# An encoder with routed experts: the router's products turned round, five weight tiles loaded earlier, the experts in another order

## The chip, the cores and the metric

The kernel runs on one core of a Trainium2 chip. The metric is the device time of one execution in microseconds (us), the median of several runs. Five engines share the work: PE multiplies matrices into eight banks of PSUM, DVE and ACT work elementwise, POOL sets zeros, SP issues the DMAs that bring weights from memory. Each engine runs its own instructions in order and waits on semaphores for the others.

## What is computed

Two layers; each adds a token mixer (four groups of heads, then `W_out`) to the 256 x 1024 activations and then a feed-forward part. In layer 0 that is dense, in layer 1 it is eight experts of which every token takes two:

```python
def reference(x, ...):
    for i in range(DEPTH):                                  # DEPTH = 2
        h = rms_norm(x, norm1_g[i])
        x = x + token_mixer(h, w_in[i], ..., w_out[i])      # 4 groups, group norm, @ w_out
        h = rms_norm(x, norm2_g[i])
        x = x + (swiglu(h, ffn_w_gate[0], ffn_w_up[0], ffn_w_down[0]) if i % 2 == 0 else
                 moe_swiglu(h, moe_w_router[0], moe_w_gate[0], moe_w_up[0], moe_w_down[0]))
    return rms_norm(x, final_norm_g)

def moe_swiglu(x, w_router, w_gate, w_up, w_down):          # x: 256 x 1024, 8 experts of 3584
    logits = xt @ w_router
    top_v, top_i = lax.top_k(logits, 2)
    gates = jax.nn.softmax(top_v, axis=-1)
    combine = sum(one_hot(top_i, 8) * gates[..., None], axis=1)
    for e in range(8):
        y = y + combine[:, e:e+1] * ((silu(xt @ w_gate[e]) * (xt @ w_up[e])) @ w_down[e])
    return y
```

All is float32. The eight experts' weights are 352 MB of the 423 MB that the kernel reads.

## The kernel before

**The recorded part.** Layers 0 and 1 up to the router are recorded first, and a planner (class `Plan`) then sets the order of the instructions on each engine by its own costs and by how many buffers of each kind there are; L532 is the line at which all of them are emitted. Weights that need full float32 precision are split by `split` into a rounded part `hi` (ACT) and a rest `lo` (DVE), from a tile `w` of 128 x 2048, and PE multiplies `hi` and `lo` by the parts of the activations. There are four `hi` buffers, three `lo` and one more of them (`lox`), 26 buffers `u` for everything of 128 x 512, and 8 PSUM banks `m`. In layer 1's `W_out`, group 0's weights are used whole, the other three groups' are split, two splits a group; each split feeds twelve matmuls of 512 columns.

**The router** (L1436). x is transposed by PE (four times four 128 x 128 blocks), ACT and DVE copy the transposed blocks `hT` out of PSUM, and 16 products with the eight columns of `W_router` (times the norm's weight: `wg`) give the logits in bank `lg`: `hT` is the stationary operand, `wg` the moving one. Then come a comparison on DVE for expert 0, a product `pos0` that counts tokens, a one-hot matrix `oh`, and the gather products `ga` of expert 0. Between them `idle` puts products that nobody reads.

**The experts' weights.** A tile is 128 x 4096 (2 MB). A ring of NRING = 10 tiles takes them in turn, so tile k may be issued when the last reader of tile k - 10 is done. Three buffers `r` lie where the state space tables of the mixer lay (L673, `opener`) and can be filled once these are read for the last time; five buffers `q` lie where `w`, `hi` and `lo` lay (L681, `opener_q`) and can be filled after `W_out`'s last matmul; two more belong to the experts' part. An expert has 21 tiles: seven column blocks in four units (2, 2, 2 and 1), each with gate `eg`, up `eu` and down `ed`. SP issues in the order in which the tiles are used. Units overlap: PE does `eg` and `eu` of one unit and then `ed` of the unit before.

**The experts' order.** The experts are ranked by their number of tokens, expert 0 always first. Ranks 1 to 4 (`WIDE`) have room for 96 tokens, here called B; the others, S, for 64. B's further 32 tokens are multiplied apart (`egx`, `ex`), while the weights are the same 21 tiles. `GROUPS` sets the order and which experts are gathered together (`gather`: at most 256 columns); the next group's gather runs during the last unit of the group before. It is 0 | 1, 5, 2 | 3, 6, 4 | 7, that is S | B S B | B S B | S. After each expert its result is added to x by the `sca` products.

Of the kernel before, what the change touches and what calls it, by code (L numbers as in the profile page):

```python
# [10 lines left out]
F32 = mybir.dt.float32  # L11
F32R = mybir.dt.float32r
# [6 lines left out]
P = 128  # L19
# [12 lines left out]
NE = 8  # L32
# [5 lines left out]


WIDE = (1, 2, 3, 4)  # L40
GROUPS = ((0,), (1, 5, 2), (3, 6, 4), (7,))

NU = 26
EXTRA = (0, 0, 1)
ZORDER = (("cf", "ssm", "qk", "vb", "cx"), ("cf", "qk", "vb", "ssm", "cx"))
GORDER = ((2, 0, 1, 3), (0, 2, 3, 1))
LATE = ()
# [7 lines left out]
FRONT = 3  # L55
FIRST = 0
URGENT = 30000.0
NR = 3
NQ = 5
NRING = 10  # L60
NHI = 4
NLO = 3
LATER = (1, 3)
TURN = 3
LEAD = 2
# [470 lines left out]
def build(tc, a, dbg=None, upto=99):  # L536
# [21 lines left out]
    def bank(name):  # L558
        if plan.open:
            return plan.buf("m", name)  # L560
        return ps.tile([P, 512], F32, tag="m", name=name)
# [15 lines left out]
        return sm.tile([P, 8], F32, tag="tiny", name=name, bufs=8)[:, :n]  # L577

    lasts = {}

    def in_turn(what, op):

# [8 lines left out]

    def split(src, parts=1):
        n = src.free_size()
        if plan.open:
            hi, lo = plan.buf("hi", "hi"), plan.buf("lo", "lo")
        else:
            hi = hl.tile([P, 1024], F32R, tag="hi", name="hi", bufs=NHI)
            lo = hl.tile([P, 1024], F32R, tag="lo", name="lo", bufs=NLO)
        hi, lo = hi[:, :n], lo[:, :n]
        for i in range(0, n, n // parts):  # L600
            c = slice(i, i + n // parts)
            in_turn("split", A.activation(hi[:, c], src[:, c], AF.Copy))
            V.tensor_tensor(lo[:, c], src[:, c], hi[:, c].bitcast(F32), ALU.subtract)
        return hi, lo
# [42 lines left out]
    def idle(after, columns):  # L647

        for n in columns:
            PE.matmul(bank("idle")[:, 0:n], ident, cst[:, 0:n], start=True, stop=True)  # L650
            plan.after(plan.ops[-1], after)
# [19 lines left out]
    right = []  # L671

    def opener():  # L673
# [4 lines left out]
            s.tile = right[0].tile([P, 4096], F32, tag=f"r{i}", name="r")  # L678
        plan.kinds["oh"][0].tile = right[0].tile([P, 4 * P], F32R, tag="oh", name="oh")

    def opener_q():  # L681

        pw.close()
        pool = ctx.enter_context(tc.tile_pool(name="qp", bufs=1, side="right", reuse_waits="tile"))
        right.append(pool)
        for i, s in enumerate(plan.kinds["q"]):
            s.tile = pool.tile([P, 4096], F32, tag=f"q{i}", name="q")
# [3 lines left out]
    def kind(name, n, w, dt=F32, pool=hp, tag=None, **kw):  # L691
        plan.kind(name, [pool.tile([P, w], dt, name=f"{name}{i}", **({"tag": tag} if tag else {}), **kw) for i in range(n)])
# [2 lines left out]
    hl = pw.enter_context(tc.tile_pool(name="hl", bufs=4))  # L695
    ring = pw.enter_context(tc.tile_pool(name="ring", bufs=4))
    kind("w", 4, 2048, pool=ring, tag="w")
    kind("hi", NHI, 1024, F32R, hl, "hi", bufs=NHI)
    kind("lo", NLO, 1024, F32R, hl, "lo", bufs=NLO)
    kind("m", 8, 512, F32, ps, "m")  # L700
    for n, w, dt, more in (("w", 2048, F32, EXTRA[0]), ("hi", 1024, F32R, EXTRA[1]), ("lo", 1024, F32R, EXTRA[2])):
        plan.more(n, [hl.tile([P, w], dt, name=f"{n}x{i}", tag=f"{n}x{i}", bufs=1) for i in range(more)])
    tables = {"el": 4096, "qr": 2048, "qi": 2048, "mt": 2048}
    for n, w in tables.items():
        kind(n, 1, w, pool=sx)
# [1 line left out]
        kind(n, 1, KD * S, F32R, top)  # L707
    plan.later("r", NR, plan.like["el"], opener)
    plan.later("oh", 1, plan.like["hi"][:, 0:4 * P], opener)
    plan.later("q", NQ, plan.like["el"], opener_q)  # L710
    kind("j", 1, 512, BF16, sm, "junk", bufs=1)
    u = lambda i: hp.tile([P, 576], F32, name="u", tag=f"u{i}")
# [266 lines left out]
    def mixer(L, T, late):  # L979
# [367 lines left out]
        groups = {}  # L1347
        for gi, f in ((3, state_space), (2, conformer), (0, attention), (1, short_conv)):
            groups[gi] = f()
        for gi in GORDER[L]:  # L1350
            group_out(gi, groups[gi])
        for t in range(2):
# [83 lines left out]
    def router():  # L1436
# [4 lines left out]
        plan.after(plan.ops[-1], early["router"])  # L1441
        wg = u2("wgr", 64).rearrange("p (k e) -> p k e", e=NE)
        V.tensor_tensor(wg, wr, g2.unsqueeze(2).to_broadcast([P, KD, NE]), ALU.mult)
        bl = bank("lg")
        copies, rest, logits = [], [], []
        for t in range(2):
            for h in range(2):
                b = bank("hT")
                with plan.one():
                    for k in range(4):  # L1450
                        c = (4 * h + k) * P
                        PE.transpose(b[:, k * P:(k + 1) * P], x[:, t, c:c + P], ident)
                turned = plan.ops[-1]
                hT = u2("hT")
                copies.append(V.tensor_copy(hT, b) if HT[2 * t + h] == "V" else A.activation(hT, b, AF.Copy))
                with plan.one():
                    for k in range(4):
                        PE.matmul(bl[:, t * NE:(t + 1) * NE], hT[:, k * P:(k + 1) * P], wg[:, 4 * h + k],
                                  start=(h + k == 0), stop=(h + k == 4))
                logits.append(plan.ops[-1])  # L1460
                hs = slice(512 * h, 512 * h + 512)
                rest.append(A.activation(h_hi[:, t, hs], x[:, t, hs], AF.Copy))
                V.tensor_tensor(h_lo[:, t, hs], x[:, t, hs], h_hi[:, t, hs].bitcast(F32), ALU.subtract).tail = URGENT - 1500.0
# [3 lines left out]
            plan.after(op, copies[-1])  # L1467
        lg, sel = lgs[:, 0], lgs[:, 1]
        te = lambda v: v.rearrange("p (t e) -> p t e", t=2)
        V.tensor_copy(lg, bl[:, 0:16])  # L1470

        gt0, s0, q0 = u2("gt0", 16), tiny(2, "s0"), tiny(2, "q0")
# [1 line left out]
        V.tensor_tensor(te(gt0), te(lg), te(lg)[:, :, 0:1].to_broadcast([P, 2, NE]), ALU.is_gt)  # L1474
        V.tensor_reduce(s0, te(gt0), AX.X, ALU.add)
        V.tensor_scalar(s0, s0, 1.5, None, ALU.is_lt)
        idle(logits[-1], (256, 256))
        bp_ = bank("pos0")
        with plan.one():
            PE.matmul(bp_[:, 0:1], C["tri"], s0[:, 0:1], start=True, stop=True)  # L1480
# [36 lines left out]
            plan.after(op, picked)  # L1517
        parts = [x for u in range(2) for x in up_parts(weights_of(0), u)]
        w0 = []
        for i, (n, src) in enumerate(parts[:NR + NQ]):  # L1520
            w0.append(plan.keep(plan.buf("r" if i < NR else "q", n)))
            kinds = tables if i == 0 else ("w", "hi", "lo") if i == NR else ()
            held = [op for op in plan.ops if any(b.kind in kinds for b in op.bufs)]
            op = SY.dma_start(w0[i], src)
            in_turn("load", op)
            for o in held:
                plan.after(op, o)
        return h_hi, h_lo, oh, w0

    def moe(h_hi, h_lo, oh0, w0, posm, comb, rst, lgs):  # L1530
# [4 lines left out]
        ring2 = pool("ring2", 1)  # L1535
        bp = pool("bp", 1)
        b2 = pool("b2", 2)
        rp, rq = right
        g2r = g2.real()
        nring = [0]  # L1540

        def weights(parts, pieces=1):

            ws = []
            for name, src in parts:
                n, i = nring[0], nring[0] % NRING
                nring[0] += 1
                if n < len(w0):
                    ws.append(w0[n])
                    continue  # L1550
                if i < NR:
                    w = rp.tile([P, 4096], F32, tag=f"r{i}", name=name)
                elif i < NR + NQ:
                    w = rq.tile([P, 4096], F32, tag=f"q{i - NR}", name=name)
                else:
                    w = ring2.tile([P, 4096], F32, tag=f"w{i}", name=name)
                n = pieces if src is parts[-1][1] else 1
                for k in range(n):
                    c = slice(4096 // n * k, 4096 // n * (k + 1))
                    SY.dma_start(w[:, c], src[:, c])  # L1560
                ws.append(w)
            return ws
# [538 lines left out]
```

## Time and profile before

| | |
|---|---|
| median of 3 runs | 1325.83 us (1325.54 to 1326.10) |
| the profiled execution | 1324.34 us, of which the span of the trace is 1322.6 us |
| PE busy | 1276.5 us (97%) |
| weight loads on PE | 765.0 us (58%) |
| DVE, ACT busy | 476.2 us (36%), 295.9 us (22%) |
| DMA | 423.32 MB, 320 GB/s over the span, 425 to 428 GB/s in most of the 40 slices after 490 us |
| granted TensorE clock | 0.984 of full speed |

The recorded part with the router takes the first 491 us, the eight experts run to 1306 us, and the final norm and the output take the rest. An instruction on PE counts as busy from its start to its modelled end, so a share of busy time says little on how fast PE goes; what a stretch lost is seen by setting it beside the same work elsewhere in the trace. Lines of the kernel are given as L532; L221 is the line at which all calls outside the recorded part are made. `q` tiles, once refilled, bear the names of what is in them (`eg`, `eu`, `ed`).

### The profile page before, as it was taken

The numbers are of one execution on the slowest core, as the hardware profiler recorded it, in microseconds if no ns is written. First come the engines' busy times: TensorE is split into PE (matmuls) and PEld (weight loads), VectorE is DVE, ScalarE is ACT, GpSimd is POOL, SyncE is SP. The second block draws the span as 40 slices with busy tenths as digits, with TensorE's granted clock in tenths as the row PEclk, the third lists the DMA queues.
The fourth block names the chain that finished last, engine by engine and source line by source line (L and its number), as shares of the span: only waits on it lengthen the run. The fifth ranks groups of instructions, "written<-read, shape, count | busy, mean of one in ns | idle before, by whom it ended". The sixth has DMA issues, their size and how long they took to land.

```text
span 1322.6 us, 23222 instructions
## 1 busy us (share of the span) xinstructions
PE 1276.5 (97%) x10172; PEld 765.0 (58%) x10173; DVE 476.2 (36%) x1059; ACT 295.9 (22%) x479; POOL 2.2 (0%) x25
## 2 busy tenths in 40 slices
PE   7999999999999999999999979999999999999995
PEld 6787799999888783444453324454445343445332
DVE  7999899855688852001001001001100100100102
ACT  4065644444535531001001000010100100100101
POOL 0000000000000000000000000000000000000000
PEclk9999899999999979999999989999999999999998
DMA  8214244555546569999999999999999999999994
GB/s 273 108 65 151 97 160 166 188 191 189 180 139 144 224 255 427 427 427 425 425 426 426 428 426 426 425 426 396 384 380 427 427 426 427 425 427 425 427 425 164
DMA packets 45923, 423.32 MB, mean 320 GB/s; under 512 B 12024, under 2 KB 14968, under 8 KB 16888
## 3 DMA queue, kind: packets, MB, share of 16 engines
q1 hardware_dynamic: 45816, 421.77, 78.5%
q8 instruction: 82, 1.34, 0.4%
q14 instruction: 25, 0.20, 0.0%
HBM read 420.21 MB, written 1.54 MB: 319 GB/s over the span
## 4 chain that ended last, share of the span: by engine, by line
PE 80%; DMA 11%; DVE 6%; ACT 2%; issue 1%; SPq 0%; DVEq 0%; ACTq 0%
PE m L532 29%; PE egu L221 25%; PE ea L221 11%; DMA eu<-in_moe_w_up 8%; PE egx L221 7%; PE ex L221 4%; DVE u L532 3%; DMA ed<-in_moe_w_down 3%; PE aT L221 1%; PE ga L221 1%; PE sca L221 1%; DVE t L532 1%; DVE lo L532 1%; ACT u L532 0%; ACT j L532 0%
## 5 line engine op out<-in xcount | busy, mean ns | idle before, releaser
L221 PE MATMUL ea<-ed,af 128*64 128x512 f32 x896 | 207.5, 602 | 3.5 <-DMA ed<-in_moe_w_down 3.5
L221 PE MATMUL egu<-eu,ef 128*64 128x512 f32 (+1 forms) x960 | 189.7, 537 | 5.1 <-DMA eu<-in_moe_w_up 5.1
L221 PE MATMUL egu<-eg,ef 128*64 128x512 f32 (+1 forms) x960 | 190.4, 540 | 3.6 <-DMA eg<-in_moe_w_gate 3.5
L221 DVE SCALAR_TENSOR_TENSOR sg<-egu,rs,sg 128x512 f32<-128x512 f32 (+1 forms) x32 | 21.9, 684 | 415.5 <-PE egu L221 399.6
L221 PEld LDWEIGHTS egu<-eg,ef 128*64 128x64 f32 x960 | 70.3, 138 | 116.9 <-issue 103.8
L221 PEld LDWEIGHTS egu<-eu,ef 128*64 128x64 f32 x960 | 69.8, 137 | 115.1 <-issue 96.8
L532 PE MATMUL m<-hlo,hi 128*128 128x256 f32 x480 | 134.7, 281 | 1.3 <-DVE hlo L532 1.3
L532 PE MATMUL m<-hh,hi 128*128 128x256 f32 x480 | 135.5, 282 | 0.0
L532 ACT ACTIVATE hi<-w 128x1024 fp32r<-128x1024 f32 x98 | 103.7, 1059 | 107.7 <-PE m L532 107.2
L221 PEld LDWEIGHTS ea<-ed,af 128*64 128x64 f32 x896 | 60.8, 137 | 113.4 <-issue 109.1
L532 DVE TENSOR_TENSOR lo<-w,hi 128x1024 fp32r<-128x1024 f32 x74 | 90.2, 1223 | 42.0 <-ACT hi L532 40.9
L532 PE MATMUL m<-hh,lo 128*128 128x256 f32 x364 | 102.2, 281 | 0.0
L532 PE MATMUL m<-hi,u 128*128 128x512 f32 x288 | 95.6, 398 | 0.0
L532 PEld LDWEIGHTS m<-hlo,hi 128*128 128x128 f32 x480 | 91.1, 190 | 2.1 <-DVE hlo L532 1.5
L532 PEld LDWEIGHTS m<-hh,hi 128*128 128x128 f32 x480 | 90.9, 189 | 1.0 <-issue 0.4
L532 DVE TENSOR_TENSOR u<-u 128x512 f32<-128x512 f32 (+5 forms) x136 | 78.8, 617 | 6.4 <-ACT u L532 4.8
L221 ACT ACTIVATE af<-aT 128x512 f32<-128x512 f32 (+2 forms) x48 | 21.4, 480 | 237.4 <-PE aT L221 237.4
L221 ACT ACTIVATE sg<-egu,rs 128x512 f32<-128x512 f32 (+1 forms) x32 | 20.3, 634 | 230.7 <-PE egu L221 230.7
L532 PEld LDWEIGHTS m<-hh,lo 128*128 128x128 f32 x364 | 69.2, 190 | 0.0
L532 PEld LDWEIGHTS m<-hi,u 128*128 128x128 f32 x288 | 54.5, 189 | 11.4 <-ACT hi L532 0.2
L532 DVE SCALAR_TENSOR_TENSOR u<-u,pp 128x256 f32<-128x256 f32 (+1 forms) x142 | 59.0, 481 | 1.5 <-ACT u L532 1.3
L532 PE MATMUL m<-u,w 128*128 128x256 f32 x256 | 58.7, 381 | 0.0
(194 smaller groups left out, 1324.0 us busy)
## 6 DMA issues: line engine op xcount, KB each, us to landing
ed<-in_moe_w_down SPq DMA_DIRECT2D x55, 2048.0 KB, 27.0
eg<-in_moe_w_gate SPq DMA_DIRECT2D x52, 2048.0 KB, 27.5
eu<-in_moe_w_up SPq DMA_DIRECT2D x52, 2048.0 KB, 30.7
w<-in_w_in SPq DMA_DIRECT2D x18, 1024.0 KB, 5.2
w<-in_ffn_w_gate SPq DMA_DIRECT2D x11, 1024.0 KB, 4.7
w<-in_ffn_w_up SPq DMA_DIRECT2D x11, 1024.0 KB, 5.1
w<-in_ffn_w_down SPq DMA_DIRECT2D x11, 1024.0 KB, 4.8
w<-in_w_out SPq DMA_DIRECT2D x8, 1024.0 KB, 5.2
```

Source lines behind the costliest of these rows:

```text
L221: return f(*[real(v) for v in a], **{k: real(v) for k, v in kw.items()})
L532: f(*[real(v) for v in a], **{k: real(v) for k, v in kw.items()})
```

## The change

Four things are changed.

1. In the router `wg` becomes the stationary operand (8 columns) and `hT` the moving one (128 columns), so the logits come out transposed, 8 x 256, in bank `lgT`. DVE copies each half to `lT`, and PE transposes it back into `lg`. One more pair of `idle` products is put in.
2. The buffers for the experts' first eight tiles are four `r`, one `p` and three `q` instead of three `r` and five `q`. `p` lies where a second set of split buffers (`hib`, `lob`) lies, which is given up earlier than the rest.
3. The split buffers become two sets of two (`hi`, `lo` and `hib`, `lob`) that `split` uses in turn; once layer 1's mixers are recorded (`few`), only the first set is used, so its `W_out` has two `hi` and two `lo`. There are 24 buffers `u` instead of 26, and the extra `lo` is gone.
4. `GROUPS` becomes 0 | 1, 2, 5 | 3, 6, 4 | 7, that is S | B B S | B S B | S.

```diff
-GROUPS = ((0,), (1, 5, 2), (3, 6, 4), (7,))
+GROUPS = ((0,), (1, 2, 5), (3, 6, 4), (7,))
-NU = 26
-EXTRA = (0, 0, 1)
+NU = 24
-NR = 3
-NQ = 5
+NR = 4
+NP = 1
+NQ = 3
-NHI = 4
-NLO = 3
+NSPLIT = 2
...
     def split(src, parts=1):
         n = src.free_size()
-        if plan.open:
-            hi, lo = plan.buf("hi", "hi"), plan.buf("lo", "lo")
-        else:
-            hi = hl.tile([P, 1024], F32R, tag="hi", name="hi", bufs=NHI)
-            lo = hl.tile([P, 1024], F32R, tag="lo", name="lo", bufs=NLO)
-        hi, lo = hi[:, :n], lo[:, :n]
+        kind_ = "" if len(few) > 0 else "ab"[nsplit[0] % 2].replace("a", "")
+        nsplit[0] += 1
+        hi, lo = plan.buf("hi" + kind_, "hi")[:, :n], plan.buf("lo" + kind_, "lo")[:, :n]
...
+    def opener_p():
+        pwb.close()
+        pool = ctx.enter_context(tc.tile_pool(name="pp", bufs=1, side="right", reuse_waits="tile"))
+        right.append(pool)
+        for i, s in enumerate(plan.kinds["p"]):
+            s.tile = pool.tile([P, 4096], F32, tag=f"p{i}", name="p")
...
+    pwb = ExitStack()
+    hlb = pwb.enter_context(tc.tile_pool(name="hlb", bufs=NSPLIT))
+    kind("hib", NSPLIT, 1024, F32R, hlb, "hib", bufs=NSPLIT)
+    kind("lob", NSPLIT, 1024, F32R, hlb, "lob", bufs=NSPLIT)
...
             groups[gi] = f()
+        few.extend([L] * L)
         for gi in GORDER[L]:
             group_out(gi, groups[gi])
...
-        bl = bank("lg")
+        bl, blT, lT = bank("lg"), bank("lgT"), u2("lT", 256)
...
-                        PE.matmul(bl[:, t * NE:(t + 1) * NE], hT[:, k * P:(k + 1) * P], wg[:, 4 * h + k],
-                                  start=(h + k == 0), stop=(h + k == 4))
+                        PE.matmul(blT[0:NE, t * P:(t + 1) * P], wg[:, 4 * h + k], hT[:, k * P:(k + 1) * P],
+                                  start=(h + k == 0), stop=(h + k == 4), skip_group_check=True)
...
+        for t in range(2):
+            V.tensor_copy(lT[0:NE, t * P:(t + 1) * P], blT[0:NE, t * P:(t + 1) * P])
+            if t:
+                idle(logits[-1], (256, 256))
+            PE.transpose(bl[:, t * NE:(t + 1) * NE], lT[0:NE, t * P:(t + 1) * P], ident[0:NE, 0:NE])
+        turned_back = plan.ops[-1]
         V.tensor_copy(lg, bl[:, 0:16])
...
-        idle(logits[-1], (256, 256))
+        idle(turned_back, (256, 256))
...
-        for i, (n, src) in enumerate(parts[:NR + NQ]):
-            w0.append(plan.keep(plan.buf("r" if i < NR else "q", n)))
-            kinds = tables if i == 0 else ("w", "hi", "lo") if i == NR else ()
+        for i, (n, src) in enumerate(parts[:NR + NP + NQ]):
+            w0.append(plan.keep(plan.buf("r" if i < NR else "p" if i < NR + NP else "q", n)))
+            kinds = {0: tables, NR: ("hib", "lob"), NR + NP: ("w", "hi", "lo")}.get(i, ())
```

Since the planner runs anew with other numbers of buffers, the order changes in many places of the recorded part. Three of them are shown.

SP's issues at the end of the recorded part, before (`r` and `q` are the experts' first tiles, `wr` is `W_router`, `ed` the first tiles of the two buffers of the experts' part):

```order
L532 DMA w_85<-in_w_out 128x2048
L532 DMA r<-in_moe_w_gate 128x4096 x2
L532 DMA r<-in_moe_w_up 128x4096
L532 DMA wr<-in_moe_w_router 128x8x8
L532 DMA q<-in_moe_w_up 128x4096
L532 DMA q<-in_moe_w_gate 128x4096 x2
L532 DMA q<-in_moe_w_up 128x4096 x2
L221 DMA ed<-in_moe_w_down 128x4096 x2
```

and of the changed kernel:

```order
L531 DMA w_85<-in_w_out 128x2048
L531 DMA r<-in_moe_w_gate 128x4096 x2
L531 DMA r<-in_moe_w_up 128x4096 x2
L531 DMA wr<-in_moe_w_router 128x8x8
L531 DMA p<-in_moe_w_gate 128x4096
L531 DMA q<-in_moe_w_gate 128x4096
L531 DMA q<-in_moe_w_up 128x4096 x2
L220 DMA ed<-in_moe_w_down 128x4096 x2
```

The tiles are the same and stand in the same order; five instead of three are in buffers that do not wait for the end of `W_out`.

ACT's last instructions of layer 1's `W_out`, before (`hi<-w` is the first half of a split; the number behind `hi` is the buffer, that behind `w` the tile of weights):

```order
L532 ACTIVATE hi_90<-w_87 128x1024
L532 ACT_TABLE_LOAD
L532 ACTIVATE u<-m_96,pp 128x256 x2
L532 ACTIVATE u<-u 128x512
L532 ACTIVATE u<-u,pp 128x256 x2
L532 ACTIVATE hi_91<-w_87 128x1024
L532 ACTIVATE u<-u 128x512
L532 ACTIVATE hi_89<-w_85 128x1024
L532 ACTIVATE u<-u,pp 128x256 x2
L532 ACTIVATE hi_88<-w_85 128x1024
L532 ACTIVATE u<-u,pp 128x256 x2
L532 ACTIVATE hh_108<-x 128x512 x2
```

and of the changed kernel:

```order
L531 ACT_TABLE_LOAD
L531 ACTIVATE u<-m_99,pp 128x256 x2
L531 ACTIVATE u<-u 128x512
L531 ACTIVATE u<-u,pp 128x256 x2
L531 ACTIVATE u<-u 128x512
L531 ACTIVATE hi_89<-w_87 128x1024
L531 ACTIVATE u<-u,pp 128x256 x2
L531 ACTIVATE hi_88<-w_87 128x1024
L531 ACTIVATE hi_89<-w_85 128x1024
L531 ACTIVATE u<-u,pp 128x256 x2
L531 ACTIVATE hi_88<-w_85 128x1024
L531 ACTIVATE hh_111<-x 128x512 x2
```

The last four splits had four buffers and have two; the first of them moved behind the work for the group's norm.

PE at the router, before (`m<-cst,x` are the transposes of x, `m<-u 128x8` the products for the logits, `m<-cst` the products that nobody reads, `m<-t,cst` is `pos0`; behind the arrow the moving operand stands first):

```order
L532 MATMUL m_99<-cst,x 128x128 x4
L532 MATMUL m_98<-u 128x8 x16
L532 MATMUL m_102<-cst 128x256
L532 MATMUL m_101<-cst 128x256
L532 MATMUL m_97<-t_152,cst 128x1 x3
L532 MATMUL m_95<-cst 128x128
L532 MATMUL m_96<-cst 128x128
L221 MATMUL ga<-oh,x 128x64 x14
```

and of the changed kernel:

```order
L531 MATMUL m_105<-cst,x 128x128 x4
L531 MATMUL m_101<-u 8x128 x16
L531 MATMUL m_102<-cst,u 128x8
L531 MATMUL m_103<-cst 128x256
L531 MATMUL m_102<-cst,u 128x8
L531 MATMUL m_106<-cst 128x256
L531 MATMUL m_100<-cst 128x256
L531 MATMUL m_99<-cst 128x256
L531 MATMUL m_104<-t_155,cst 128x1 x3
L531 MATMUL m_105<-cst 128x128
L531 MATMUL m_101<-cst 128x128
L220 MATMUL ga<-oh,x 128x64 x14
```

Ahead of `pos0` there stand two small transposes and four instead of two products that nobody reads. (An operation of this list on float32 shows as two instructions in the trace.)

## Rows read from the trace of the kernel before

**Rows 1.** Windows, one expert each: engines' busy us (instructions), PEclk, DMA share, GB/s.

```profile
490.99:570.15 79.16, 79.16 (x420) 32.05 (x420) 12.58 (x55) 7.05 (x12) 0.00 (x0) 0.98 1.01 426
570.15:689.21 119.06, 117.45 (x1183) 53.27 (x1182) 8.34 (x16) 8.75 (x19) 0.00 (x0) 1.00 1.01 426
689.21:776.70 87.49, 83.15 (x441) 30.95 (x438) 7.12 (x11) 6.53 (x12) 0.00 (x0) 0.98 1.01 426
776.70:901.79 125.09, 121.14 (x1159) 55.39 (x1158) 11.95 (x23) 8.75 (x19) 0.00 (x0) 0.99 1.01 426
901.79:1019.63 117.84, 117.84 (x1223) 54.83 (x1221) 9.21 (x18) 9.58 (x21) 0.00 (x0) 1.00 0.94 393
1019.63:1099.36 79.73, 79.73 (x441) 30.06 (x437) 7.12 (x11) 6.53 (x12) 0.00 (x0) 1.00 1.01 426
1099.36:1220.56 121.20, 118.88 (x1160) 55.49 (x1159) 9.64 (x19) 8.75 (x19) 0.00 (x0) 1.00 1.01 426
1220.56:1306.33 85.77, 85.77 (x480) 34.43 (x476) 7.28 (x12) 6.53 (x12) 0.00 (x0) 1.00 0.93 393
```

**Rows 2.** The chain that ended last, experts: start us, us, what.

```profile
589.21 7.04 PE egx L221 x128
...
797.53 7.04 PE egx L221 x128
...
896.30 2.08 PE ga L221 x16
...
903.68 1.33 PE rs L221 x53
...
917.17 7.04 PE egx L221 x128
...
964.93 13.73 PE egu L221 x64
...
1077.79 31.73 DMA eu<-in_moe_w_up
...
1116.65 7.04 PE egx L221 x128
```

**Rows 3.** The page's costliest groups on PE: busy us, mean ns, idle before, releaser.

```profile
L221 PE MATMUL ea<-ed,af 128*64 128x512 f32 x896 | 207.5, 602 | 3.5 <-DMA ed<-in_moe_w_down 3.5
L221 PE MATMUL egu<-eu,ef 128*64 128x512 f32 (+1 forms) x960 | 189.7, 537 | 5.1 <-DMA eu<-in_moe_w_up 5.1
L221 PE MATMUL egu<-eg,ef 128*64 128x512 f32 (+1 forms) x960 | 190.4, 540 | 3.6 <-DMA eg<-in_moe_w_gate 3.5
```

**Rows 4.** SP's timeline at layer 1's W_out: start us, us, issue.

```profile
440.19 1.31 SPq L532 DMA_DIRECT2D r<-in_moe_w_gate  x2
...
474.67 0.33 SPq L532 DMA_DIRECT2D q<-in_moe_w_up  x1
```

**Rows 5.** The page's split groups on ACT and DVE: busy us, mean ns, idle before.

```profile
L532 ACT ACTIVATE hi<-w 128x1024 fp32r<-128x1024 f32 x98 | 103.7, 1059 | 107.7 <-PE m L532 107.2
...
L532 DVE TENSOR_TENSOR lo<-w,hi 128x1024 fp32r<-128x1024 f32 x74 | 90.2, 1223 | 42.0 <-ACT hi L532 40.9
```

**Rows 6.** PE's timeline, end of W_out and router: start us, us, operation.

```profile
471.31 0.39 PE L532 MATMUL m<-lo,u 128*128 128x512 f32 x1
...
474.03 0.39 PE L532 MATMUL m<-lo,u 128*128 128x512 f32 x1
...
476.23 3.64 PE L532 MATMUL m<-u 128*128 128x8 f32 x32
...
479.72 1.11 PE L532 MATMUL m<-cst 128*128 128x256 f32 x4
...
482.85 6.08 PE L221 MATMUL ga<-oh,x 128*128 128x64 f32 x28
```

**Rows 7.** Windows at the router, columns as in rows 1.

```profile
474.26:481.00 6.74, 6.74 (x56) 6.28 (x55) 3.78 (x9) 5.51 (x13) 0.00 (x0) 1.00 0.82 297
481.00:494.70 13.70, 13.70 (x58) 11.11 (x59) 4.82 (x31) 1.96 (x3) 0.00 (x0) 0.50 1.01 429
```

More of the change, by code (lines that the diff above doesn't have):

```diff
@@ L579, in build @@
     lasts = {}
+    nsplit, few = [0], []
     def in_turn(what, op):
@@ L697, in build @@
     kind("w", 4, 2048, pool=ring, tag="w")
-    kind("hi", NHI, 1024, F32R, hl, "hi", bufs=NHI)
-    kind("lo", NLO, 1024, F32R, hl, "lo", bufs=NLO)
+    kind("hi", NSPLIT, 1024, F32R, hl, "hi", bufs=NSPLIT)
+    kind("lo", NSPLIT, 1024, F32R, hl, "lo", bufs=NSPLIT)
+    pwb = ExitStack()
+    hlb = pwb.enter_context(tc.tile_pool(name="hlb", bufs=NSPLIT))
+    kind("hib", NSPLIT, 1024, F32R, hlb, "hib", bufs=NSPLIT)
+    kind("lob", NSPLIT, 1024, F32R, hlb, "lob", bufs=NSPLIT)
     kind("m", 8, 512, F32, ps, "m")
-    for n, w, dt, more in (("w", 2048, F32, EXTRA[0]), ("hi", 1024, F32R, EXTRA[1]), ("lo", 1024, F32R, EXTRA[2])):
-        plan.more(n, [hl.tile([P, w], dt, name=f"{n}x{i}", tag=f"{n}x{i}", bufs=1) for i in range(more)])
     tables = {"el": 4096, "qr": 2048, "qi": 2048, "mt": 2048}
@@ L709, in build @@
     plan.later("oh", 1, plan.like["hi"][:, 0:4 * P], opener)
+    plan.later("p", NP, plan.like["el"], opener_p)
     plan.later("q", NQ, plan.like["el"], opener_q)
@@ L1537, in moe @@
         b2 = pool("b2", 2)
-        rp, rq = right
+        rp, rp2, rq = right
         g2r = g2.real()
@@ L1552, in weights @@
                     w = rp.tile([P, 4096], F32, tag=f"r{i}", name=name)
-                elif i < NR + NQ:
-                    w = rq.tile([P, 4096], F32, tag=f"q{i - NR}", name=name)
+                elif i < NR + NP:
+                    w = rp2.tile([P, 4096], F32, tag=f"p{i - NR}", name=name)
+                elif i < NR + NP + NQ:
+                    w = rq.tile([P, 4096], F32, tag=f"q{i - NR - NP}", name=name)
                 else:
```

## The prediction

> **What bounds the kernel now.** I read first the windows that hold one expert each [rows 1]. The column DMA share stands at 1.01 and the last column at 426 GB/s in all but two, so the stream of weights never pauses while the experts run; a tile of 2,097 KB takes 4.92 us and an expert's 21 tiles 103.4 us. PE needs less than that for an S (79.73 us where nothing was late, the window from 1019.63) and more for a B (117.84, from 901.79). So neither engine bounds the stage by itself: during an S the weights are late, during a B they run ahead until the ring of ten tiles is full. (In the last window, also at 393, the stream ends.) The reader is to see both in two odd windows: S from 689.21 lasts 87.49 instead of 79.73, and in the second of the two adjacent B's the stream falls to 393 GB/s, which is 117.84 x 33/426 = 9.1 us of lost transfer.
>
> The chain [rows 2] then says how long PE waited. A B's first gate and up products last 13.73 us, and 15.38 where the small `rs` products lie among them (901.79 to 917.17). The other three B's took 19.06 (570.15 to 589.21, with `rs`), 20.83 (776.70 to 797.53) and 17.29 (1099.36 to 1116.65, both without): waits of 3.7, 7.1 and 3.6 us. With the S's 87.49 - 79.73 = 7.8 that is 22.2 us of waiting for weights.
>
> The idle column shows only 3.5 + 5.1 + 3.6 = 12.2 us of it [rows 3], because a matmul that waits can count as busy. The Trainium skill warns of this (Perfetto Trace Analysis, Identifying the Most-Contended Engine): busy time of matmuls is a poor measure of how near PE is to its limit. By the 97% busy share and that column, weights that are never late would be worth 12.2 us at most; by the windows it is 22.2. The trace agrees with the rule, and I go by the windows.
>
> **Order and early tiles, together.** The instructions of an expert stay the same; what moves is when its weights are there. Before, SP issued three tiles at 440 us and the other five at 474.67, after `W_out`'s last matmul [rows 4]. Five tiles take 24.6 us and the gap is 34.5, so two more tiles fit in, and the stream of the experts stands 2 x 4.92 = 9.8 us further at any moment at which nothing holds it back. The first B, which waited 3.7 us, then waits no more, with 6 us to spare.
>
> PE's ledger, with the first product at 490.99 as before: S 79.16; B 119.06 - 3.7 = 115.4; second B 117.84 - 1.3 = 116.5, since `rs` (1.33) falls away inside a group [rows 2]. That ends at 802.1. Is the stream in front by then? By itself it would have 5 + (802.1 - 474.67)/4.92 = 71.5 tiles, with 63 used. In the kernel before, the tile for which the last B waited (the 130th, landed at 1077.79 + 31.73 = 1109.52) landed 89.9 us or 18.3 tiles after the end of the adjacent B's at 1019.63, so 111.7 had landed there with 105 used: 6.7 ahead is what the ring allows. 8.5 is more; the ring is full here too, and the stream leaves 802.1 as it left 1019.63. From there the same tile of the next B (after one S) lands at 802.1 + 89.9 = 892.0; PE, with the gather that now stands in that S (2 x 2.08, [rows 2]), asks for it at 802.1 + 83.9 + 8.5 = 894.5 (8.5 is 15.38 less half of 13.73), so nothing is late. B 115.4 and S 79.7 bring PE to the last B at 1081.1 and to its up products at 1088. Their tile lands 42 tiles after 892.0, at 1098.6, and PE waits 10.6 us. Before, it landed at 1109.5. What follows (this B, the last S, the norm) is unchanged, so this part is worth **-10.9 us**. Everything up to 802.1 is PE alone; whatever moves the first product at 490.99 moves the end by as much.
>
> **Split buffers in `W_out`.** Four splits there now share two buffers. While PE uses one buffer's twelve matmuls, 2.72 us (471.31 to 474.03, [rows 6]), the other must be filled: ACT 1.06 and DVE 1.22 us, 2.28 [rows 5], plus two hand-overs and whatever DVE and ACT do between. It nearly fits. Bounds: 0 if it fits, 4 x 2.28 = 9.1 if each split is waited for whole. I take **+2**, half a microsecond each. It delays `q` and the first product alike.
>
> **Router.** The loads of 128 stationary columns go, and 128 moving columns come. Before, 32 instructions took 3.64 us, 0.114 each; of 256 columns one takes 1.11/4 = 0.28 [rows 6], so one of 128 takes at most 0.14: 0 to +0.8, I take +0.2, near the lower end since the tail of the last product is in the 1.11. Behind it PE's queue holds one more pair of products that nobody reads (1.1 us) and two small transposes (0.2) ahead of `pos0`; the two DVE copies run beside them. Queued behind are `pos0`, `oh` and all of `ga`, so it counts in full: +1.5 together. The clock was granted at 0.50, that is 1.2 GHz, from 481.0 to 494.7, after PE had spent 3.64 us on products of eight columns; before that it was 1.00 [rows 7]. What the fuller logits do to that lies between 0 (it falls as before) and -6.8 (it does not fall: half of 13.7). I take **-1.8**: the fall comes later by the length of the logits, half of 3.64, since the 28 thin `ga` products follow and the clock did not rise during them.
>
> **The rest of the recorded part** is planned anew with two `u` fewer and split sets used in turn. No row prices this; I take 0 and keep the whole of it for the rivals.
>
> **Sum.** -10.9 + 2 + 1.5 - 1.8 = -9.2. The profiled execution took 1324.34 (its span 1322.6 and 1.7 around it): 1315.1 by its own measure. It lies 1.5 us below the median of 1325.83, so the forecast for a median is **1316.6 us**, and by itself 1312 to 1321.
>
> **Rivals.**
> - *The clock stays at its full level.* For it: it stood at 1.00 through all the dense stages and fell only behind the thin logits. Against it: `ga` is thin too and follows. The Trainium skill (TensorE: Matmul & The Clock Gate, Part 1) says that the gate answers to how active the array has been; the granted clock falling behind the thin products agrees. The sum is then -10.9 + 2 + 1.5 - 6.8 = -14.2: 1311.6.
> - *The change does not do what it says: the five tiles are not there in time.* `p` waits for `hib` and `lob`, which are read in `W_in` products that PE uses as filling, and `q` stands behind it on SP. If it comes with `q`, the first B waits its 3.7 again: -5.5, 1320.3. For it: PE still does such products in `W_out`. Against it: there are 34.5 us for 24.6.
> - *The split sets in fixed turn cost time everywhere, and the kernel gets slower.* Place: the 98 splits of both layers and the dense part. ACT waited 107.2 us for PE before them, that is for a buffer to come free [rows 5]; now a split waits for its own set even if one of the other is free, and PE waits behind it. From 0.12 us a split (11.9 us) on the kernel is slower beyond what can be measured; at 0.15 it is +14.7 - 9.2 = +5.5: 1331. Against it: buffers come free in the order in which they were filled as long as one stream of products uses them.
> - *The same at 0.07 to 0.12 us a split, or the same sum from fewer `u`*: the gain is eaten up, 1323 to 1328.5.
>
> **Numbers.** Chances: forecast 0.46, full clock 0.18, late tiles 0.10, gain eaten up 0.16, slower 0.10. What a measurement of this kernel can tell from no change is about 0.2%, 2.65 us. The first three lie below 1323.2: faster 0.74; same 0.16; slower 0.10. The range runs from 1309.5, which takes in the full clock, to 1327, which takes in most of the case in which the gain is eaten up; some 2 in 10 are left out.
>
> **What would show it.** In the profile after: five tiles issued before `W_out`'s end; the windows of the S and two B's in front at about 79, 115 and 116.5 us with no wait for a DMA; lost transfer (below 426 GB/s) in the third expert instead of the fifth; the one wait, some 10 us, at the last B. The first expert product tells the recorded part and the router apart from all this: 491 plus 1.7 by the forecast. The argument on the ring is wrong if PE waits for weights in the S behind the two B's; the clock's term is read from the granted clock over the gather of expert 0; and if the first product comes after 500 the rivals on the splits decide.

## The result, and the profile after

The changed kernel takes 1311.45 us (median of 4 runs, 1311.21 to 1312.22), the kernel before on the same chip 1325.68 (1325.19 to 1326.10): a ratio of 0.989, 95% interval 0.988 to 0.991, so 14.2 us faster. The forecast was 1316.6 with a range of 1309.5 to 1327. The time is inside the range, but what came about is the rival in which the clock stays at its full level (1311.6).

First the windows of one expert each, in the changed kernel (columns as in [rows 1]: from:to, length, PE busy, PEld, DVE, ACT, POOL, clock, DMA share, GB/s):

```profile
488.90:566.24 77.34, 77.34 (x418) 31.77 (x420) 12.66 (x55) 7.06 (x12) 0.00 (x0) 1.00 1.00 426
566.24:681.46 115.22, 115.22 (x1184) 53.32 (x1182) 8.34 (x16) 8.76 (x19) 0.00 (x0) 1.00 1.01 426
681.46:797.65 116.19, 116.19 (x1167) 53.07 (x1165) 8.92 (x15) 9.60 (x21) 0.00 (x0) 1.00 0.97 410
797.65:881.88 84.23, 84.23 (x473) 33.83 (x471) 11.02 (x21) 6.53 (x12) 0.00 (x0) 1.00 1.01 426
881.88:997.06 115.18, 115.18 (x1184) 52.59 (x1182) 8.34 (x16) 8.75 (x19) 0.00 (x0) 1.00 1.01 426
997.06:1081.77 84.71, 80.70 (x440) 30.25 (x437) 7.12 (x11) 6.53 (x12) 0.00 (x0) 1.00 1.01 427
1081.77:1207.37 125.60, 120.82 (x1158) 55.25 (x1159) 9.63 (x19) 8.75 (x19) 0.00 (x0) 0.99 1.01 426
1207.37:1293.14 85.77, 85.76 (x480) 34.43 (x476) 7.28 (x12) 6.53 (x12) 0.00 (x0) 1.00 0.91 386
```

The reader is to see three things. The two B's in front last 115.22 and 116.19, so neither waits. The stream slackens in the third expert (410 GB/s) and no longer in the fifth: 116.19 x 16/426 = 4.4 us are lost there, where [rows 1] lost 9.1. And PE waits in one place only, at the last B: the S ahead of it takes 84.71 where [rows 1] has 79.73, 5.0 too long, and the chain names the two tiles that were late (start us, us, what):

```profile
1024.46 32.66 DMA ed<-in_moe_w_down
1057.24 39.10 DMA eu<-in_moe_w_up
1096.38 7.08 PE egu L220 x30
1103.46 7.04 PE egx L220 x128
```

From 1081.77 to 1103.46 are 21.69, and an unhurried start of a B takes 13.73 [rows 2]: 8.0 more. Together PE waits 12.9 us, where it waited 22.2 before. The `eu` tile landed at 1096.34; before it was 1109.52 [rows 2].

The page's idle column, against [rows 3], shows 8.8 us of these 12.9:

```profile
L220 PE MATMUL ea<-ed,af 128*64 128x512 f32 x896 | 204.9, 598 | 2.5 <-DMA ed<-in_moe_w_down 2.5
L220 PE MATMUL egu<-eg,ef 128*64 128x512 f32 (+1 forms) x960 | 188.9, 540 | 4.6 <-DMA eg<-in_moe_w_gate 4.6
L220 PE MATMUL egu<-eu,ef 128*64 128x512 f32 (+1 forms) x960 | 186.7, 536 | 1.7 <-DMA eu<-in_moe_w_up 1.7
```

At the router, windows of the changed kernel over the same stretches as [rows 7]:

```profile
474.26:481.00 6.74, 6.37 (x53) 4.91 (x51) 3.72 (x8) 5.96 (x15) 0.00 (x0) 1.00 0.84 305
481.00:494.70 13.70, 13.24 (x91) 9.38 (x91) 6.48 (x37) 1.87 (x3) 0.00 (x0) 1.00 1.01 429
```

and PE's timeline there (start us, us, engine, operation; `128*8` is the stationary operand):

```profile
474.44 1.91 PE L531 MATMUL m<-cst,x 128*128 128x128 f32 x16
476.28 1.91 PE L531 MATMUL m<-u 128*8 128x128 f32 x16
478.57 1.91 PE L531 MATMUL m<-u 128*8 128x128 f32 x16 [0.37 <-DVE u L531]
...
484.19 3.31 PE L220 MATMUL ga<-oh,x 128*128 128x64 f32 x28 [0.16 <-DVE oh L531]
487.33 0.79 PE L531 MATMUL m<-lgs,cst 128*128 128x8 f32 x6
487.98 0.64 PE L220 MATMUL ga<-oh,x 128*128 128x64 f32 x4
488.90 3.65 PE L220 MATMUL egu<-r,ef 128*64 128x512 f32 x16 [0.29 <-PE ga L220]
```

The granted clock stays at 1.00 (2.4 GHz) where it was 0.50. The 28 gather products take 3.31 instead of 6.08 us [rows 6], although they begin 1.3 us later.

SP's issues of the first tiles, against [rows 4] (start us, us):

```profile
438.80 1.92 SPq L531 DMA_DIRECT2D r<-in_moe_w_gate  x2
440.81 0.86 SPq L531 DMA_DIRECT2D r<-in_moe_w_up  x2
...
451.50 7.79 SPq L531 DMA_DIRECT2D p<-in_moe_w_gate  x1
474.41 0.33 SPq L531 DMA_DIRECT2D q<-in_moe_w_gate  x1
```

Five tiles are issued long before the end of `W_out`, and `q` comes 35.6 us behind the first `r`, where it came 34.5 behind before.

### The profile page after: what moved, and what is told of

It is laid out like the page before. It is cut to its first block, busy times and chain, and to the rows that moved or that the text cites. A ratio compares the mean times of both kernels' runs of the same rounds, so it can differ in the third digit from the quotient of the medians.

```text
span 1309.4 us, 23257 instructions
## 1 busy us (share of the span) xinstructions
PE 1267.5 (97%) x10178; PEld 756.9 (58%) x10179; DVE 476.8 (36%) x1061; ACT 295.5 (23%) x480; POOL 2.2 (0%) x25
## 4 chain that ended last, share of the span: by engine, by line
PE 84%; DVE 7%; DMA 6%; ACT 2%; issue 1%; SPq 0%; DVEq 0%; ACTq 0%
PE m L531 28%; PE egu L220 27%; PE ea L220 14%; PE egx L220 8%; DVE u L531 4%; PE ex L220 4%; DMA eu<-in_moe_w_up 3%; DMA ed<-in_moe_w_down 2%; PE aT L220 1%; DVE t L531 1%; PE ga L220 1%; PE sca L220 1%; ACT j L531 0%; DVE lo L531 0%; ACT u L531 0%
## 5 line engine op out<-in xcount | busy, mean ns | idle before, releaser
L531 DVE TENSOR_TENSOR lo<-w,hi 128x1024 fp32r<-128x1024 f32 x52 | 63.6, 1224 | 33.5 <-ACT hi L531 33.2
L531 PE MATMUL m<-hlo,hi 128*128 128x256 f32 x240 | 67.7, 282 | 0.8 <-DVE hlo L531 0.8
L531 ACT ACTIVATE hi<-w 128x1024 fp32r<-128x1024 f32 x52 | 55.0, 1058 | 59.3 <-PE m L531 58.1
L531 PE MATMUL m<-hh,hi 128*128 128x256 f32 x240 | 68.3, 284 | 0.0
L531 PE MATMUL m<-hh,lo 128*128 128x256 f32 x240 | 67.5, 281 | 0.0
L531 PE MATMUL m<-hh,hib 128*128 128x256 f32 x240 | 67.2, 280 | 0.0
L531 PE MATMUL m<-hlo,hib 128*128 128x256 f32 x240 | 66.9, 279 | 0.0
L531 PE MATMUL m<-hh,lob 128*128 128x256 f32 x240 | 66.9, 279 | 0.0
L531 DVE TENSOR_TENSOR lob<-w,hib 128x1024 fp32r<-128x1024 f32 x46 | 56.3, 1223 | 20.9 <-ACT hib L531 20.8
L531 ACT ACTIVATE hib<-w 128x1024 fp32r<-128x1024 f32 x46 | 48.7, 1059 | 58.1 <-PE m L531 58.1
```

The source lines that it names most:

```text
L531: f(*[real(v) for v in a], **{k: real(v) for k, v in kw.items()})
```

## The experiments

The theory after the result had two halves. First, a ledger (a running account of PE's time and of the stream's): until the ring has once been full, in two adjacent B's, the stream of weights runs at its own pace, and whatever PE gains ahead of a wait is lost in that wait; from the full ring on, a shift of PE's moves the end. Second, the turned logits keep the clock up. The rivals: all parts simply add; or the clock stays up for another reason. All times below stand against runs of the kernel before in the same series (medians 1325.9 to 1326.3); where the changed kernel is named, it is its 1311.45 from the series above, in which the kernel before had 1325.68.

**1. The router alone, put into the kernel before.**

```diff
-                        PE.matmul(bl[:, t * NE:(t + 1) * NE], hT[:, k * P:(k + 1) * P], wg[:, 4 * h + k],
+                        PE.matmul(blT[0:NE, t * P:(t + 1) * P], wg[:, 4 * h + k], hT[:, k * P:(k + 1) * P],
...
+            PE.transpose(bl[:, t * NE:(t + 1) * NE], lT[0:NE, t * P:(t + 1) * P], ident[0:NE, 0:NE])
...
```

> The kernel before, with the router's new products and the extra pair of idle products alone. Theory of the ledger: the granted clock stays at 1.00 over the gather and the first expert's products, the first B's weights are asked for about 3.6 us earlier (first product and first expert together), but the first B waits for its weights in the kernel before (3.7 us) and its tile lands when it landed, so the wait grows by the same 3.6 and the end does not move: 0 us, -1 to +1. Rival, the router counts in full wherever it stands: -3.6 us. Rival, the clock stays up for another reason (the planner's new order of W_out): it falls at about 481 as before, and the router costs its fillers, 0 to +1.5 us.

1325.88 us in 11 runs, 1325.93 before in 15: ratio 1.0002 (0.9993 to 1.0011). The clock nevertheless did what it does in the changed kernel; its window at the router:

```profile
481.00:494.70 13.70, 13.31 (x96) 9.88 (x96) 6.97 (x38) 3.67 (x9) 0.00 (x0) 1.00 1.01 428
```

and this is where the gain went, the chain at its first B:

```profile
513.61 31.18 DMA ed<-in_moe_w_down
544.90 39.09 DMA eu<-in_moe_w_up
...
591.12 7.04 PE egx L221 x128
```

In this execution `q` was issued at 476.46 and the first B's `egx` began 114.7 us later; before it is 589.21 - 474.67 = 114.5 [rows 2, 4]. PE came earlier and waited longer. Both rivals are refuted: the router does not count in full here, and no new order in `W_out` is needed for the clock.

**2. The order of the experts alone, in the kernel before.**

```diff
-GROUPS = ((0,), (1, 5, 2), (3, 6, 4), (7,))
+GROUPS = ((0,), (1, 2, 5), (3, 6, 4), (7,))
```

> The kernel before with the new order of the experts alone. Theory of the ledger: the first B waits 3.7 us as before, the second B follows without a wait, the ring fills there, and the up tile of the last B lands about 7.2 us earlier (3.7 less than the 10.9 of order and early tiles together): -7.2 us, -5 to -8. Rival, the order does nothing by itself because each expert still has 21 tiles and the stream is the limit: 0 us, the waits only change places. Rival, the order carries the whole of what was put down to order and tiles: -10.9 us.

1320.22 us, ratio 0.995 (0.994 to 0.997): -5.7. The mechanism is the ledger's, which had put it at 7.2. The third expert and the last late tile:

```profile
690.76:806.97 116.21, 116.21 (x1167) 53.10 (x1165) 8.93 (x15) 9.59 (x21) 0.00 (x0) 1.00 0.99 417
```

```profile
1066.63 39.10 DMA eu<-in_moe_w_up
```

The tile landed at 1105.73, 298.8 us behind the end of the adjacent B's at 806.97. The prediction had 1098.6 - 802.1 = 296.5 for this interval; in the changed kernel it is 1096.34 - 797.65 = 298.7. Since the stream runs at 426 or 427 GB/s all through this interval, the lead that the full ring leaves was put 2.2 us too large; why it is smaller here than in the kernel before isn't shown.

**3. The changed kernel with the old order** (the diff of 2 reversed).

> The changed kernel with the old order of the experts. Theory of the ledger: the two early tiles take the wait from the first B, the S and B behind the second place still wait, with the stream 9.8 us further, and the ring is full at the two adjacent B's in the fifth place; from there all is as in the kernel before, 10 us earlier: -10 us against the kernel before, +4.3 against the changed one. Rival, the gain is router and clock and the early tiles bring nothing without the order: -3.6 us against before. Rival, early tiles and router add up in full: -13.4 us against before, the order then being worth 1.

1315.38 us, ratio 0.992 (0.991 to 0.994): -10.5, as the ledger has it. The order is worth 3.9 here and 5.7 in 2. The interval of 2 reaches from 4.2 to 8.0, so these two runs alone don't show that the parts don't add; experiments 1 and 4 do.

**4. The changed kernel with the old router** (the diff of 1 reversed, with the added idle pair taken out).

> The changed kernel with the old router (transposed x stationary, one pair of idle products). Theory of the ledger: PE waits for no weights before the ring is full in the second B, so what the router costs counts in full: the granted clock falls to 0.50 over the gather again, the first product comes about 2 us later, the first expert takes 79.2 instead of 77.3, and the end comes 3.6 to 4 us later than in the changed kernel (-10.5 against the kernel before). Rival, the stream hides it as in a bound stage: 0 against the changed kernel. Rival, the clock stays at 1.00 because of what stands ahead of the router now, and the kernel becomes faster by the fillers and transposes left out: -1 to -1.5 against the changed kernel.

1315.77 us, ratio 0.993 (0.992 to 0.994): 4.3 slower than the changed kernel. Its window and its gather:

```profile
481.00:494.70 13.70, 13.70 (x54) 10.31 (x56) 4.81 (x31) 1.29 (x3) 0.00 (x0) 0.50 1.01 429
```

```profile
481.73 6.15 PE L220 MATMUL ga<-oh,x 128*128 128x64 f32 x28
```

The same router that is worth nothing in 1 is worth 4.3 here, where no wait lies between it and the full ring.

**5. Without the added pair of idle products.**

```diff
-            if t:
-                idle(logits[-1], (256, 256))
```

> The changed kernel without the extra pair of idle products; the logits stay turned round. Theory, the orientation of the logits keeps the clock: the granted clock stays at 1.00 from 474 to 504, the gather takes 3.3 us, and the end moves by 0 to -1.1 us (1.1 us is what the pair costs at most; part of it lies beside the comparisons on DVE). Rival, the extra pair keeps it: the clock falls to 0.50 over the gather as in the kernel before, gather 6.1 us, and the end comes 3 to 4.3 us later than in the changed kernel.

1311.60 us, ratio 0.990 (0.988 to 0.992), the clock in the window from 481.00 to 494.70 at 1.00. So the turned logits keep the clock without the pair, in the execution that was profiled. One of the four executions took 1315.31 us at a mean clock of 0.988, where those of the changed kernel stand at 0.990 to 0.993; it has no profile, so whether the clock fell in it stays open. Of the pair's 1.1 us, 0.5 show between `q` and the first product (14.0 instead of 14.5), which is too little to be seen in the time.

**6. The old logits with both idle pairs behind them.**

```diff
...
-        idle(turned_back, (256, 256))
+        idle(logits[-1], (256, 256, 256, 256))
```

> The changed kernel with the old logits (transposed x stationary, eight moving columns) but with both pairs of idle products behind them. Theory, the orientation decides: the clock falls to 0.50 as with the old router, and the end comes 4.3 to 5.4 us later than in the changed kernel (the fall, as measured, and up to 1.1 for the second pair). Rival, four idle products hold the clock up: it stays at 1.00 over the gather, and the end is within 1 us of the changed kernel's.

Neither expectation: the executions are of two kinds, 1319.2 and 1320.3 us with a mean granted clock of 0.984 and 0.983, and 1309.1, 1309.5 and 1312.4 with 0.991 or 0.992. The profiled one is of the first kind, and in it the clock had fallen during the eight-column products themselves:

```profile
474.26:481.00 6.74, 6.74 (x51) 6.61 (x50) 4.52 (x9) 5.96 (x15) 0.00 (x0) 0.83 0.84 308
481.00:494.70 13.70, 13.70 (x58) 12.80 (x58) 5.06 (x33) 1.16 (x1) 0.00 (x0) 0.50 1.02 434
```

There the first product of the experts comes 494.31 - 474.37 = 19.9 us behind `q` instead of 14.5, and from it to the first B's `egx` it is 95.2 us instead of 92.7: together the 7.9 by which this kind is slower than the changed kernel. In the faster kind the old logits cost nothing: 1309.1 and 1309.5 lie below the changed kernel's 1311.2 to 1312.2, in another series.

**7. Idle products between the old logits**, one of 256 columns behind each of the first three groups, and one pair behind all.

```diff
...
+                if logits:
+                    plan.after(plan.ops[-1], gap)
                 logits.append(plan.ops[-1])
+                if len(logits) < 4:
+                    idle(logits[-1], (256,))
+                    gap = plan.ops[-1]
...
```

> The changed kernel with the old logits (transposed x stationary, eight moving columns), but with one idle product of 256 columns behind each of the first three groups of them; the one pair behind all logits stays as before. Theory, the clock answers to how full the products are over a stretch and not to the orientation: with the idle products between, 1.6 us in all, it stays at 1.00 over the gather, and the end lies within 1.5 us of the changed kernel's, -1 to +1. Rival, thin products let the clock fall whatever stands between them: it falls to 0.50 by the gather, and the end comes 4.3 to 6 us later. Between the two: it falls in some executions, with both values in the times, as with both pairs behind the logits (1309 and 1320).

Again two kinds, as the last of the expectations has it: now four of 1310.3 to 1311.5 us (clock 0.990 to 0.993) and two of 1317.4 and 1320.3 (0.985, 0.984); the profiled one is of the second, with 0.50 from 481.00 to 494.70. So, to judge by times and mean clocks, full-width products beside the thin ones can hold the clock, but not in every execution; the turned logits held it over the gather's 28 products in all nine profiles that have them. The Trainium skill (TensorE: Matmul & The Clock Gate, Part 1) has the clock follow how busy the engine has recently been. If busy is read from PE's busy column, the rows differ from that, and they decide: the column stands at 6.74 of 6.74 us in the stretch in or behind which the clock falls, and at 6.37 where it doesn't fall.

**8. Early tiles undone, first attempt**: the fourth tile ordered behind `W_out` in the planner.

```diff
-            kinds = {0: tables, NR: ("hib", "lob"), NR + NP: ("w", "hi", "lo")}.get(i, ())
+            kinds = {0: tables, NR - 1: ("hib", "lob", "w", "hi", "lo")}.get(i, ())
```

> The changed kernel, but with the fourth and fifth tile issued only after the last matmul of W_out, as before; buffers, planned order, router and the experts' order stay. Theory of the ledger: the stream stands two tiles (9.8 us) back until the ring fills, the first B waits again, now for about 7 us (3.7 and the 3.6 by which PE asks earlier), and the router's gain is lost in that wait: the end is that of the order alone, -5.7 us against the kernel before, +8.5 against the changed kernel. Rival, the tiles matter only as far as PE waits in the kernel before: +3.7. Rival, the earlier tiles collide with W_out and cost there what they bring: 0 or below against the changed kernel, and the recorded part ends earlier.

1311.74 us, ratio 0.989 (0.988 to 0.991), and the edit missed its aim: it moved the issue in SP's order, but the buffer is free early and nothing made SP wait for `W_out`:

```profile
441.15 12.44 SPq L531 DMA_DIRECT2D r<-in_moe_w_up  x1
453.68 1.15 SPq L531 DMA_DIRECT2D p<-in_moe_w_gate  x1
474.34 0.33 SPq L531 DMA_DIRECT2D q<-in_moe_w_gate  x1
```

It tests none of its three theories. It shows only that the fourth tile may be issued 12 us later at no cost that can be seen.

**9. Early tiles undone by the buffers**: both sets of split buffers with `w`, three `r` and five `q`.

```diff
-NR = 4
-NP = 1
-NQ = 3
+NR = 3
+NP = 0
+NQ = 5
...
-    pwb = ExitStack()
+    pwb = pw
...
```

> The changed kernel with three r buffers and five q as before, so that the fourth and fifth tile can only be loaded after the last matmul of W_out (both sets of split buffers then lie with w); router, split sets in turn, number of u and order of the experts stay as changed. Theory of the ledger: the first B waits for its weights again, about 7 us (3.7 as before and the 3.6 by which PE asks earlier), the router's gain is lost in that wait, and the end is that of the order alone, about 1319 to 1320 us (+8 against the changed kernel), less 1.4 by which this recorded part ends earlier. Rival, PE waits for these tiles only as long as in the kernel before: +3.7 against the changed kernel. Rival, early tiles bring nothing: 0.

1318.89 us, ratio 0.995 (0.993 to 0.996): 7.4 slower than the changed kernel, as the ledger has it. `q` with the fourth tile is issued at 474.18, and the first B waits:

```profile
542.16 39.09 DMA eu<-in_moe_w_up
...
588.37 7.04 PE egx L220 x128
```

where the changed kernel has 581.61; of the 6.8 us, 1.6 are the clock, which fell for a while behind the gather in this execution (last section), and the rest is the wait. The two tiles are worth more than the 3.7 us that PE waited for them before, because without them the router's gain goes into the same wait.

**10. A ring of nine tiles.**

```diff
-NRING = 10
+NRING = 9
```

> The changed kernel with a ring of nine tiles instead of ten. Theory, the full ring at the two adjacent B's sets where the stream leaves them, and with it the one wait at the last B: with one tile less the stream leaves one tile (4.92 us) later, the third expert's transfer loses more (its window falls below the 412 and 380 GB/s of the changed kernel's slices), and the end comes 5 to 6 us later than in the changed kernel. Rival, the ring is never full there and the wait at the last B comes from the stream alone: 0 to +1 us.

1317.65 us, ratio 0.994 (0.992 to 0.996): 6.2 slower. The third expert:

```profile
682.93:799.13 116.20, 116.20 (x1167) 53.07 (x1165) 8.93 (x15) 9.60 (x21) 0.00 (x0) 1.00 0.95 397
```

PE takes the same 116.2 us, and the stream loses 116.2 x 29/426 = 7.9 us instead of 4.4. The ring is full there, and what it can't take comes back as waits in both B's that follow, the fifth expert and the last B, and in the S between them:

```profile
860.19 33.51 DMA eu<-in_moe_w_up
...
900.83 7.04 PE egx L220 x128
...
1063.89 38.80 DMA eu<-in_moe_w_up
...
1109.81 7.04 PE egx L220 x128
```

The changed kernel has these two `egx` at 897.25 and 1103.46. At the end of the third expert this execution is 799.13 - 797.65 = 1.5 us behind it, which goes with the short fall of the clock behind the gather that it has too; at the fifth expert 3.6, at the last B 6.4. So 4.9 us come back behind the full ring, the time of one tile (4.92).

**11. The old order of the experts, gathered otherwise.**

```diff
-GROUPS = ((0,), (1, 2, 5), (3, 6, 4), (7,))
+GROUPS = ((0,), (1, 5), (2, 3, 6), (4, 7))
```

> The changed kernel with the experts in the old order, S B S B B S B S, but gathered as S | B S | B B S | B S. Theory of the ledger: in the old grouping a gather with its rs products (some 5 us of PE) stands between the two adjacent B's, where PE is the limit and the ring is full; here each gather lies in an S, where PE waits for weights anyway, so the two B's shorten by it: -5 to -6 us against the same order in the old grouping (1315.4), about 1310, 1 to 2 us below the changed kernel. Rival, the place of a gather doesn't matter and only the order of B and S does: 1315.4, as with the old order. Rival, all that counts is the sum of the tiles and both orders end together: 1311.5.

1309.12 us (1308.64 to 1309.28), ratio 0.987 (0.986 to 0.989), with experiment 12 the fastest version here; the changed kernel had 1311.21 to 1312.22, in another series, and the intervals of the two ratios overlap. Its windows from the third expert to the fifth:

```profile
681.89:767.12 85.23, 84.42 (x472) 33.79 (x469) 11.03 (x21) 6.53 (x12) 0.00 (x0) 1.00 1.01 427
767.12:888.75 121.63, 117.85 (x1183) 53.18 (x1182) 8.34 (x16) 8.76 (x19) 0.00 (x0) 1.00 1.01 426
888.75:1005.89 117.14, 116.60 (x1167) 53.03 (x1165) 8.92 (x15) 9.59 (x21) 0.00 (x0) 1.00 0.97 410
```

and of experiment 3, the same order of experts in the old grouping:

```profile
682.20:766.69 84.49, 80.33 (x440) 29.96 (x437) 7.12 (x11) 6.53 (x12) 0.00 (x0) 1.00 1.01 427
766.69:892.66 125.97, 122.21 (x1158) 55.68 (x1160) 11.95 (x23) 8.76 (x19) 0.00 (x0) 0.97 1.01 426
892.66:1010.33 117.67, 117.67 (x1224) 54.50 (x1221) 9.22 (x18) 9.60 (x21) 0.00 (x0) 1.00 0.94 392
```

The gather has moved out of the first of the adjacent B's into the S ahead of them. That S hardly grows (85.23 after 84.49), because it waited for weights anyway; the B loses 4.3 us, and the stream in the second B is at 410 instead of 392. The places of the gathers alone are worth 1315.4 - 1309.1 = 6.3 us.

**12. The same without the added idle pair** (the diffs of 5 and 11).

> The grouping S | B S | B B S | B S together with the turned logits without the extra pair of idle products. Theory of the ledger: in this order PE waits for weights at the third and fourth expert, ahead of the full ring, so 0.5 us less before the first product changes nothing: as the grouping alone, 0 to -0.5. Rival, the gains add: -0.5 to -1 against the grouping alone. Rival, without the idle pair the clock falls in some executions: +2 to +4 in these.

1308.99 us (1307.95 to 1310.34), ratio 0.987 (0.985 to 0.989): the same as 11. That agrees with the ledger, but the first rival's 0.5 us can't be told apart from it.

## Why the prediction was right, and where not

*Order and early tiles, -10.9.* Right in mechanism: no wait in front, the ring full in the third expert, one wait left at the last B (12.9 us; the sum had 10.6). Experiment 4, which has these parts and the old router, is the nearest measurement. From `q` to the last B's `egx` it takes 1107.66 - 473.82 = 633.84 us, before 1116.65 - 474.67 = 641.98 [rows 2, 4]: -8.1. Of the 2.8 missing, 2.2 are the lead of the full ring (experiment 2).

*Split buffers in `W_out`, +2.* From the first `r` to `q` it takes 35.6 us, before 34.5: +1.1. In the ten other profiles with the new split buffers it is 35.6 to 35.7, in the two others with the old ones 34.5. The stretch holds more than the four splits, so this is what it cost as a whole.

*The rest of the recorded part, 0.* It was not 0: the first `r` is issued at 438.80, before at 440.19 [rows 4], -1.4; over all profiles it is 438.2 to 439.6 with the new buffers (eleven) and 440.2 to 442.0 with the old (three). With the +1.1 the recorded part up to `q` is as long as before (474.41 and 474.67), so nothing is seen of the rivals in which the new plan made it slower. Which of the edits shortens the part ahead of the first `r` was not tried apart.

*Router, +1.5.* From the first logits to the gather it takes 484.19 - 476.28 = 7.9 us, before 482.85 - 476.23 = 6.6 [rows 6]: +1.3. The clock shortens `pos0` and the idle products behind it by 1.0 of that (1.25 to 0.72 and 1.20 to 0.69), so at an unchanged clock it would be +2.3.

*Clock, -1.8.* This is the step that failed: "the fall comes later by the length of the logits, half of 3.64, since the 28 thin `ga` products follow". The fall did not come later; it did not come. The gather and what follows it up to the first product take 488.90 - 484.19 = 4.7 us where they took 8.1 [rows 6], -3.4; the first expert takes 77.34 instead of 79.16 [rows 1], -1.8; with the 1.0 above that is -6.2, close to the bound of -6.8 that the prediction had given to a rival with a chance of 0.18. Experiments 1 and 4 show that the router does it, and 5 that the turned products do it without the added pair, with one execution of four left open. What the prediction said for that rival was too strong: the clock did not fall "only behind the thin logits". [rows 1] has 0.98 for the S from 689.21, and there the granted clock was 0.52 from 771.00 to 774.00, after PE had been busy for 0.80 of the 3.00 us ahead, waiting for weights. What it said against it, the thin gather, may have been worth something: see the last section.

*The sum.* The profiled span fell by 13.2 us. Up to `q` it is -0.3, and from `q` to the last B's `egx` (1103.46 - 474.41 = 629.05, before 641.98) -12.9; of these, -8.1 are experiment 4's, and the remaining -4.8 come with the router and the clock. The rows of router and clock give 3.9 of them (1.3 - 3.4 - 1.8); of the other 0.9, 0.8 lie in the first B, which takes 116.0 us in experiment 4 and 115.2 in the changed kernel, for a reason that the traces don't show. After the last B's `egx` nothing moved. The forecast of -9.2 was smaller because the clock's term was 4.4 too small, which the 2.8 too much in the first term made up in part. That the time came so near the forecast, and nearer still to the full-clock rival's 1311.6, is partly luck: errors of several us cancel in both sums.

*What moves the end.* That "whatever moves the first product at 490.99 moves the end by as much" holds in the changed kernel (experiment 4) and not in the kernel before (experiment 1): there every early microsecond ends in the first B's wait. The prediction said this only of the changed kernel; experiment 9, in which the first B waits again without the early tiles, shows what makes it true.

## What to carry to other kernels

Where a stream of weights runs through a ring beside compute-bound and stream-bound stages, find the place where the ring is full. A gain ahead of a wait for the stream is worth nothing, the same gain ahead of the full ring counts in full, and side work belongs into the stages that wait for the stream. Where products with a small moving operand stand ahead of dense work, look at the granted clock behind them, and try the small operand as the stationary one. All of this is from one kernel.

## Not expected of the hardware

- With eight-column products and idle products behind or between them the times fall into two kinds, as if the clock fell in one execution and not in the next: 1309 and 1320 us from one program (experiment 6). A single profile shows one kind only; of the faster kind none was taken, so its clock is known only by its mean over the execution (0.991 or 0.992, and 0.983 or 0.984 in the slower kind).
- With the turned logits the clock can still fall for about 3 us, behind the gather. It does so in four of the nine profiles that have them, those of experiments 8, 9, 10 and 12; the first expert's first products then take 5.3 us instead of 3.65. In experiment 9:

```profile
488.61 5.27 PE L220 MATMUL egu<-r,ef 128*64 128x512 f32 x16  [0.29 <-PE ga L220]
```
